# A transformer-and-experts layer on one core: the last expert place becomes a small one

## Chip, core and metric

The kernel runs on one core of a Trainium2 chip. The metric is device time in microseconds of one execution; lower is better. Engines: TensorE (PE, its weight loads PEld), VectorE (DVE), ScalarE (ACT), GpSimd (POOL), SyncE (SP, which issues most loads), and the core's 16 DMA engines.

## What is computed

One layer over 1024 tokens of width 1024: two token mixers (SSD and windowed attention), an output projection, and a mixture of 32 SwiGLU experts, each token in two of them, then a final RMSNorm. Only the end of it matters here:

```python
x = x + g1 * (jnp.concatenate([ssd_x, attn_x], axis=-1) @ w_out[layer])
h2 = rms_norm(x, norm2[layer]) * (1 + sc2) + sh2
...
def expert_block(args):
    xb, e = args
    return (jax.nn.silu(xb @ w_gate[e]) * (xb @ w_up[e])) @ w_down[e]
...
out = jax.ops.segment_sum(y_buf.astype(f32) * w_buf[:, None], tok_buf, num_segments=n_tok + 1)
...
x = x + g2 * moe_x.reshape(b, n_tok, d)
...
return rms_norm(x, norm_final)
```

The weights of an expert are 6 MB in f32 (gate, up, down); all 32 experts are read.

## The kernel before

After the mixers, `moe()` works through 32 *places*, one expert each. Which expert stands at which place is found on the chip: experts 0 to 2 keep places 0 to 2, the others are sorted by their count of tokens, and `ranks()` gives the smallest counts to the places in `HALVES`. Those are the *small* places: a block of up to 64 tokens, whose rows of 1024 are handled as two half rows of 512, so that 128 partitions are filled. A small place multiplies in plain f32 straight from the loaded weights `wf` (`half_gu` L1261, `half_down` L1285). All others are *full*: 128 tokens, and every weight tile is taken apart into two fp32r parts, `wh` by a cast on ScalarE (L179) and `wl` by a subtraction on VectorE (L180), with three matmuls for each product (`gu` L1320, `down` L1346). Tokens beyond a place's block go through a loop with a count found at run time (`moe_rest`).

Names of a place's steps: gathered tokens `xe` are transposed (`pxe`), gate and up go to PSUM `pgu`, ScalarE makes `sg` (`sgh` in a small place), VectorE the gated product `hg` (L1328; `hgh`, L1268), which is transposed (`phT`) into `hT`; down goes to `py`; VectorE scales it into `ye` (L1352; `yeh`, L1290), and POOL adds these rows into the tensor `acc` in HBM by an indirect DMA (L1356; L1294). `schedule()` writes the steps down: gate and up of place p stand between the down steps of place p-1, except where a place is apart (the last one is: place 30's down is done before place 31's gate and up). Within that, a scheduler orders each engine's instructions; an engine runs its own in that order.

Weights come in pieces of 1 MB, each place's six in the order of use, into two rings of 7 and 6 (`prefetch`); SyncE issues them in order and waits when no slot is free.

The end: `final()` gathers the rows of `acc` that the last place's tokens need (`ya`) and loads the eight blocks of 128 rows of `acc` (`yf`, SyncE). These wait until the adds of places 0 to 30 have landed. `final_rows()` normalises each block (square and sum on ScalarE L1538, root L1539, reciprocal L1540 and multiplication L1541 on VectorE) and writes it to the output (L1566). The last place is not added into `acc`: its product `ye` (L1568) is added to `ya` (L1569), normalised, and its rows are scattered over the written output (L1571), after the last of the eight writes.

Of the kernel before, what the change touches and what calls it, by code (L numbers as in the profile page):

```python
# [9 lines left out]
F32 = mybir.dt.float32  # L10
F32R = mybir.dt.float32r
BF = mybir.dt.bfloat16
I32 = mybir.dt.int32
AF = mybir.ActivationFunctionType
OP = mybir.AluOpType
AX = mybir.AxisListType

P = 128
D = 1024
NT = 1024  # L20
# [5 lines left out]
NE = 32  # L26
# [8 lines left out]
C_ID, C_SEL, C_COS, C_SIN, C_U, C_L, C_US, C_LS, C_ONE, C_BL, C_BR, C_SELB, C_IO, C_TOK, C_RP, C_HALF = (  # L35
    0, 128, 130, 386, 642, 770, 898, 1026, 1154, 1282, 1410, 1538, 1666, 1698, 1706, 1738)
# [20 lines left out]


FIXED, MID, REST = 3, 13, 14
HALVES = (3,) + tuple(range(4, NE - 1, 2))  # L60
H = 64

TS = NT + P
# [2 lines left out]
def ranks():  # L66

    r = list(range(FIXED)) + list(HALVES) + [p for p in range(FIXED, NE) if p not in HALVES and p != MID] + [MID]
    return [r.index(p) for p in range(NE)]
# [55 lines left out]
class Kern:  # L125
# [960 lines left out]
    def overflow(self):  # L1086
# [21 lines left out]

        nh = len(HALVES)
        v.tensor_scalar(cap, rank, FIXED - 0.5, float(H - P), op0=OP.is_ge, op1=OP.mult)  # L1110
# [74 lines left out]
    def half(self, b):  # L1185

        return b == NE or b in HALVES

# [230 lines left out]
    def moe(self):  # L1419
        blocks = list(range(MID + 1)) + [NE] + list(range(MID + 1, NE))  # L1420
        at = lambda p: [p, NE] if p == MID else [p]
        X, A, T, Y, Z, G = {}, {}, {}, {}, {}, {}
        done = 0
        add = lambda b: self.half_add(Z.pop(b), b) if self.half(b) else self.y_add(Z.pop(b), self.lst[:, b, :])

        def x_ahead(p):

            nonlocal done
            for b in at(p):
                k = blocks.index(b)  # L1430
                X[b] = self.half_x(k) if self.half(b) else self.x_t(k)
                for i in range(done, min(k + 3, NE + 1)):
                    if 4 <= i + 2 < NE + 1:
                        self.lst_load(blocks[i + 2])
                    self.gather(i, self.lst[:, blocks[i], :], blocks[i])
                done = min(k + 3, NE + 1)

        for i in range(3):
            self.lst_load(i)
        for i in range(2):  # L1440
            self.gather(i, self.lst[:, i, :])
        self.g2 = self.mod_load(self.mp, 3, "g2")
        self.g2h = self.mp([512], "g2h")
        for n in range(2):
            self.nc.sync.dma_start(out=self.g2h[n * H:n * H + H], in_=self.modd[3][None, n * 512:n * 512 + 512].to_broadcast([H, 512]))
        self.counts()
        self.lst_load(3)
        done = 2
        x_ahead(0)
        for t in self.steps:  # L1450
            k, p = t[0], t[-1] if len(t) == 2 else t[1] if len(t) > 2 else None
            if k == "gu":
                if t[2] == 0:
                    for b in at(p):
                        G[b] = self.bank2(name="pgu")
                wg, wu = self.chunk(p, 2 * t[2]), self.chunk(p, 2 * t[2] + 1)
                for b in at(p):
                    if self.half(b):
                        self.half_gu(t[2], X[b], wg[0], wu[0], G[b])
                    else:  # L1460
                        self.gu(t[2], X[b], wg[1], wu[1], G[b])
            elif k == "act":
                for b in at(p):
                    A[b] = (self.half_act if self.half(b) else self.act)(G.pop(b))
            elif k == "x":
                if p + 1 < NE:
                    x_ahead(p + 1)
            elif k == "hT":
                for b in at(p):
                    T[b] = (self.half_h if self.half(b) else self.h_t)(A.pop(b))  # L1470
                    Y[b] = self.bank2(name="py")
            elif k == "down":
                w = self.chunk(p, 8 + t[2])
                for b in at(p):
                    if self.half(b):
                        self.half_down(T[b], w[0], Y[b], t[2])
                    else:
                        self.down(T[b], w[1], Y[b], t[2])
            elif k == "y":
                for b in at(p):  # L1480
                    Z[b] = self.half_y(Y.pop(b), b) if self.half(b) else self.y_out(Y.pop(b), self.lst[:, b, :])
                    if p != REST - 1:
                        add(b)
            elif k == "rest":
                self.moe_rest()
                for b in list(Z):
                    add(b)
            elif k == "final":
                self.final()
            elif k == "last":  # L1490
                self.final_rows(Y.pop(p), self.lst[:, p, :])

    def moe_rest(self):

# [35 lines left out]
            self.y_add(self.y_out(py, lst, y), lst)  # L1530
        self.xe = xe

    def norm_out(self, y):

        nc, v = self.nc, self.nc.vector
        jk = self.fp([D], "junk", 2, BF)
        st = self.sml.tile([P, 2], F32, name="xss")
        nc.scalar.activation(jk, y, AF.Square, accum_out=st[:, 0:1])  # L1538
        nc.scalar.activation(st[:, 1:2], st[:, 0:1], AF.Sqrt, bias=self.eps, scale=1.0 / D)  # L1539
        v.reciprocal(st[:, 1:2], st[:, 1:2])  # L1540
        v.scalar_tensor_tensor(y, y, st[:, 1:2], self.nf, op0=OP.mult, op1=OP.mult)  # L1541

    def final(self):

        nc = self.nc
        self.wl.close()
        self.fp = self.pool("fin", "right")
        self.nf = self.fp([D], "nf")
        nc.scalar.dma_start(out=self.nf, in_=self.a["norm_final"].to_broadcast([P, D]))
        self.rowsy = self.fp([D], "ya")  # L1550
        nc.gpsimd.indirect_dma_start(
            out=self.rowsy, out_offset=None, in_=self.acc[:, :],
            in_offset=bass.IndirectOffsetOnAxis(ap=self.lst[:, NE - 1, 1:2], axis=0),
            bounds_check=NT + P - 1, oob_is_err=False)
        ys = [self.fp([D], "yf", 8) for _ in range(NBX)]
        for b in range(NBX):
            nc.sync.dma_start(out=ys[b], in_=self.acc[b * P:(b + 1) * P, :])
        self.ys = ys

    def final_rows(self, py, lst):  # L1560

        nc, v = self.nc, self.nc.vector
        outw = []
        for b in range(NBX):
            self.norm_out(self.ys[b])
            outw.append(nc.sync.dma_start(out=self.out[b * P:(b + 1) * P, :], in_=self.ys[b]))  # L1566
        y = self.mp([D], "ye", 2)
        v.scalar_tensor_tensor(y, py, lst[:, 2:3].bitcast(F32), self.g2, op0=OP.mult, op1=OP.mult)  # L1568
        v.tensor_tensor(y, y, self.rowsy, OP.add)  # L1569
        self.norm_out(y)  # L1570
        i = nc.gpsimd.indirect_dma_start(  # L1571
            out=self.out, out_offset=bass.IndirectOffsetOnAxis(ap=lst[:, 0:1], axis=0),
            in_=y, in_offset=None, bounds_check=NT - 1, oob_is_err=False)
        for o in outw:
            self.tc.add_manual_dep(i.ins, o.ins.name, mybir.DependencyInfo(mybir.DependencyClass.Sync, mybir.DependencyReason.DATA), reason="rows written twice")
        self.fp.close()
# [147 lines left out]
```

## Time and profile before

| | |
|---|---|
| median of 3 runs | 1316.91 us (1312.76 to 1318.18) |
| the profiled execution | 1317.32 us |
| its span, first to last instruction | 1315.2 us |
| TensorE busy | 1164.3 us (89%) |
| VectorE busy | 828.8 us (63%) |
| ScalarE busy | 598.2 us (45%) |
| HBM traffic over the span | 261 GB/s |
| granted TensorE clock, mean | 0.952 of full speed |

The profile is of one execution. Times in its rows count from the start of the span; a row's idle time in brackets names what ended the wait before it. In the expert stage many rows repeat a pattern with every pair of places.

### The profile page before, as it was taken

Reading aid. Unit: us, or ns where it says so; the run is one execution under the profiler, and the core shown is the slowest. Engines: PE = TensorE matmul, PEld = TensorE weight load, DVE = VectorE, ACT = ScalarE, POOL = GpSimd, SP = SyncE. Lnnn points to the kernel's source line nnn. Section 1 sums busy time; section 2 is a strip of 40 time slices with the busy share of each in tenths; the row PEclk is TensorE's granted clock in tenths of the full one; section 3 lists DMA queues with packets and bytes.
Section 4 is the critical chain, followed back from the end, with each engine's and each line's share of the span. In section 5 each row is a group of like instructions: output and inputs, shape, how many; then the busy total and the mean of one; then the engine's idle time right before and its main releaser. Section 6 shows DMA issues by size and latency. Waiting matters only on the chain. (4 is left out here: it accounts for less than half of the span.)

```text
span 1315.2 us, 18760 instructions
## 1 busy us (share of the span) xinstructions
PE 1164.3 (89%) x6628; PEld 853.0 (65%) x6628; DVE 828.8 (63%) x1396; ACT 598.2 (45%) x1064; POOL 341.2 (26%) x290
## 2 busy tenths in 40 slices
PE   5789999888888999899946999999899999999982
PEld 2678778778876666588744766655456666555551
DVE  1688885678956977555586855455345555555455
ACT  4643333265537776533342734344324443444344
POOL 0250000467623444211432121212112222122110
PEclk9889999989988999999977999999999999999996
DMA  9655644866423400395365899999869999999965
GB/s 338 251 201 184 211 137 133 255 194 215 154 69 100 139 31 9 118 355 178 120 248 169 311 374 412 406 394 380 307 229 412 395 405 405 389 389 386 360 203 224
DMA packets 104481, 335.02 MB, mean 255 GB/s; under 512 B 19533, under 2 KB 37965, under 8 KB 79809
## 3 DMA queue, kind: packets, MB, share of 16 engines
q1 hardware_dynamic: 94672, 314.78, 64.2%
q0 software_dynamic: 9136, 17.36, 5.3%
q10 hardware_dynamic: 576, 1.66, 0.3%
q8 instruction: 53, 0.87, 0.3%
q14 instruction: 44, 0.35, 0.1%
HBM read 299.74 MB, written 43.43 MB: 261 GB/s over the span
## 5 line engine op out<-in xcount | busy, mean ns | idle before, releaser
L180 DVE TENSOR_TENSOR wl<-wf,wh 128x1024 fp32r<-128x1024 f32 x204 | 241.7, 1220 | 86.0 <-ACT wh L179 82.6
L179 ACT CAST wh<-wf 128x1024 fp32r<-128x1024 f32 x204 | 204.8, 1050 | 136.3 <-PE pgu L1320 95.9
L1261 PE MATMUL pgu<-wf,xT 128*64 128x256 f32 x1024 | 135.0, 393 | 0.4 <-DVE yeh L1290 0.4
L1320 PE MATMUL pgu<-wl,xh 128*128 128x512 f32 x272 | 96.1, 418 | 17.1 <-DVE wl L180 17.1
L1261 PEld LDWEIGHTS pgu<-wf,xT 128*64 128x64 f32 x1024 | 73.6, 139 | 50.9 <-issue 15.2
L1320 PE MATMUL pgu<-wh,xh 128*128 128x512 f32 x272 | 96.1, 427 | 10.1 <-ACT wh L179 10.0
L466 PE MATMUL pzq<-xw,hxh 128*128 128x256 f32 x512 | 99.3, 293 | 0.0
L768 POOL TENSOR_SCALAR p<-p,sst 128x640 f32<-128x640 f32 (+1 forms) x32 | 66.0, 2065 | 101.3 <-DVE sst L765 53.7
L1320 PE MATMUL pgu<-wh,xl 128*128 128x512 f32 x272 | 88.8, 407 | 0.0
L1356 POOL DMA_INDIRECT acc<-ye,lst x16 | 34.2, 2140 | 198.8 <-DVE ye L1352 188.5
L1346 PE MATMUL py<-wh,hT 128*128 128x512 f32 x272 | 81.1, 407 | 3.4 <-ACT hT L1338 3.1
L466 PEld LDWEIGHTS pzq<-xw,hxh 128*128 128x128 f32 x512 | 82.4, 195 | 1.0 <-issue 0.2
L1320 PEld LDWEIGHTS pgu<-wl,xh 128*128 128x128 f32 x272 | 53.1, 195 | 39.1 <-DVE wl L180 26.1
L1320 PEld LDWEIGHTS pgu<-wh,xh 128*128 128x128 f32 x272 | 50.5, 195 | 40.7 <-ACT wh L179 25.3
L347 PE MATMUL pxb<-hxh,xw 128*128 128x512 f32 x256 | 76.4, 397 | 0.0
L466 PE MATMUL pzq<-xw,hxl 128*128 128x256 f32 x256 | 73.8, 288 | 0.0
L751 DVE TENSOR_REDUCE sst<-psc 128x1 f32<-128x640 f32 (+1 forms) x64 | 50.4, 789 | 27.5 <-PE psc L750 22.5
L1294 POOL DMA_INDIRECT acc<-yeh,hrow x16 | 35.4, 2215 | 114.7 <-DVE yeh L1290 97.1
L1285 PE MATMUL py<-wf,hTh 128*64 128x512 f32 x256 | 63.4, 613 | 0.9 <-ACT hTh L1278 0.9
L1346 PEld LDWEIGHTS py<-wh,hT 128*128 128x128 f32 x272 | 49.4, 190 | 21.8 <-ACT hT L1338 5.5
L1320 PEld LDWEIGHTS pgu<-wh,xl 128*128 128x128 f32 x272 | 53.6, 197 | 13.3 <-issue 2.4
L1309 ACT CAST xh<-pxe 128x512 fp32r<-128x512 f32 x34 | 19.5, 589 | 93.7 <-PE pgu L1320 57.5
(347 smaller groups left out, 2523.2 us busy)
## 6 DMA issues: line engine op xcount, KB each, us to landing
wf<-in_w_gate SPq DMA_DIRECT2D x64, 1024.0 KB
wf<-in_w_up SPq DMA_DIRECT2D x64, 1024.0 KB
wf<-in_w_down SPq DMA_DIRECT2D x64, 1024.0 KB
wa<-in_w_ada SPq DMA_DIRECT2D x48, 512.0 KB
R<-csd SPq DMA_DIRECT2D x16, 512.0 KB
xl<-xd SPq DMA_DIRECT2D x17, 256.0 KB
xt<-in_x SPq DMA_DIRECT2D x8, 512.0 KB
xf<-in_w_xbc SPq DMA_DIRECT2D x8, 512.0 KB
```

The source lines that it names most:

```text
L179: self.nc.scalar.copy(hi, src)
L180: (eng or self.nc.vector).tensor_tensor(lo, src, hi.bitcast(F32), OP.subtract)
L347: nc.tensor.matmul(px[s], w(wp, kc), self.hx(hp, kc, s, 512), start=st, stop=sp)
L466: nc.tensor.matmul(ps, self.hx(hp, kc, b // 4, P, (b % 4) * P), w(wp, kc), start=kc == 0 and hp + wp == 0, stop=kc == KC - 1 and hp == 1)
L751: v.tensor_reduce(mx, ps[:, o:512 + nl], AX.X, OP.max)
L768: (v if j % 2 else nc.gpsimd).tensor_scalar(p_, p_, den[:, j - i:j - i + 1], None, op0=OP.mult)
L1261: self.nc.tensor.matmul(pg[n * H:n * H + H, o:o + 256], xT[:, i0 + kk, a * H:a * H + H], w[:, kk * 512 + n * 256:kk * 512 + n * 256 + 256] ...
L1285: self.nc.tensor.matmul(py[n * H:n * H + H, 0:512], hT[:, i, a * H:a * H + H], w[:, n * 512:n * 512 + 512], start=f == 0, stop=f == 3)
L1294: self.nc.gpsimd.indirect_dma_start(out=self.acc.rearrange("t (a c) -> (t a) c", a=2), out_offset=bass.IndirectOffsetOnAxis(ap=self.hrow[: ...
L1320: nc.tensor.matmul(pg[:, n * 512:(n + 1) * 512], x[xp][:, k, :], w[wp][:, kk * 512:(kk + 1) * 512], start=k == 0 and xp + wp == 0, stop=k ...
L1346: nc.tensor.matmul(py[:, n * 512:(n + 1) * 512], hT[:, hp, f, :], wd[wp][:, n * 512:(n + 1) * 512], start=f == 0 and hp + wp == 0, stop=f ...
L1356: self.nc.gpsimd.indirect_dma_start(out=self.acc[:, :], out_offset=bass.IndirectOffsetOnAxis(ap=lst[:, 0:1], axis=0), in_=y, in_offset=Non ...
```

## The change

The last place, 31, becomes a small one. So that there are 15 small places as before, `HALVES` goes on in steps of two up to 24, and then 27, 29, 31 (before: up to 30). Places 25 and 26 are now both full, then small and full alternate to the end. The last place's rows are half rows: gathered from `acc` by half-row numbers `hr`, summed per half (`norm_half`), the two halves' sums added by a matmul with the matrix `pair`, multiplied with the half-width norm `nfh`, and scattered as half rows.

```diff
 FIXED, MID, REST = 3, 13, 14
-HALVES = (3,) + tuple(range(4, NE - 1, 2))
+HALVES = (3, 4, 6, 8, 10, 12, 14, 16, 18, 20, 22, 24, 27, 29, 31)
...
+    def norm_half(self, y):
+
+        nc, v = self.nc, self.nc.vector
+        jk = self.fp([512], "junkh", 1, BF)
+        st = self.sml.tile([P, 2], F32, name="xss")
+        nc.scalar.activation(jk, y, AF.Square, accum_out=st[:, 0:1])
+        ps = self.bank([1], name="psum", tag="B")
+        nc.tensor.matmul(ps, self.pair, st[:, 0:1], start=True, stop=True)
+        nc.scalar.activation(st[:, 1:2], ps, AF.Sqrt, bias=self.eps, scale=1.0 / D)
+        v.reciprocal(st[:, 1:2], st[:, 1:2])
+        v.scalar_tensor_tensor(y, y, st[:, 1:2], self.nfh, op0=OP.mult, op1=OP.mult)
...
-        self.rowsy = self.fp([D], "ya")
+        self.nfh, self.pair = self.fp([D // 2], "nfh"), self.fp([P], "pair")
+        for n in range(2):
+            nc.scalar.dma_start(out=self.nfh[n * H:n * H + H], in_=self.a["norm_final"][:, n * 512:n * 512 + 512].to_broadcast([H, 512]))
+
+            nc.vector.tensor_tensor(self.pair[:, n * H:n * H + H], self.ident[:, 0:H], self.ident[:, H:P], OP.add)
+        hr = self.fp([1], "hr", 1, I32)
+        nc.vector.tensor_scalar(hr, self.lst[:, NE - 1, 1:2], 2.0, self.C[:, C_HALF:C_HALF + 1], op0=OP.mult, op1=OP.add)
+        self.rowsy = self.fp([D // 2], "ya")
         nc.gpsimd.indirect_dma_start(
-            out=self.rowsy, out_offset=None, in_=self.acc[:, :],
-            in_offset=bass.IndirectOffsetOnAxis(ap=self.lst[:, NE - 1, 1:2], axis=0),
-            bounds_check=NT + P - 1, oob_is_err=False)
+            out=self.rowsy, out_offset=None, in_=self.acc.rearrange("t (a c) -> (t a) c", a=2),
+            in_offset=bass.IndirectOffsetOnAxis(ap=hr[:, 0:1], axis=0),
+            bounds_check=2 * (NT + P) - 1, oob_is_err=False)
...
-        y = self.mp([D], "ye", 2)
-        v.scalar_tensor_tensor(y, py, lst[:, 2:3].bitcast(F32), self.g2, op0=OP.mult, op1=OP.mult)
+        y = self.half_y(py, NE - 1)
         v.tensor_tensor(y, y, self.rowsy, OP.add)
-        self.norm_out(y)
+        self.norm_half(y)
         i = nc.gpsimd.indirect_dma_start(
-            out=self.out, out_offset=bass.IndirectOffsetOnAxis(ap=lst[:, 0:1], axis=0),
-            in_=y, in_offset=None, bounds_check=NT - 1, oob_is_err=False)
+            out=self.out.rearrange("t (a c) -> (t a) c", a=2),
+            out_offset=bass.IndirectOffsetOnAxis(ap=self.hrow[:, NE - 1:NE], axis=0),
+            in_=y, in_offset=None, bounds_check=2 * NT - 1, oob_is_err=False)
```

What it moves, engine by engine (names as above; the place a row belongs to is said in the sentence). VectorE before, from place 25's `hT` to the yeh of place 26, with place 27's splits around it:

```order
L1339 TENSOR_TENSOR hT<-phT,hT 128x512
L180 TENSOR_TENSOR wl<-wf,wh 128x1024 x2
L1352 SCALAR_TENSOR_TENSOR ye<-py,lst,g_6904 128x1024
L180 TENSOR_TENSOR wl<-wf,wh 128x1024
L1268 TENSOR_TENSOR hgh<-sgh,pgu 128x256
L180 TENSOR_TENSOR wl<-wf,wh 128x1024 x4
L1200 TENSOR_SCALAR hrow<-lst,C 128x1
L1290 SCALAR_TENSOR_TENSOR yeh<-py,lst,g2h 128x512
L180 TENSOR_TENSOR wl<-wf,wh 128x1024 x3
```

VectorE now, from `hg` of place 25 to `hg` of place 26:

```order
L1328 TENSOR_TENSOR hg<-sg,pgu 128x512
L180 TENSOR_TENSOR wl<-wf,wh 128x1024 x2
L1339 TENSOR_TENSOR hT<-phT,hT 128x512
L180 TENSOR_TENSOR wl<-wf,wh 128x1024 x4
L1200 TENSOR_SCALAR hrow<-lst,C 128x1
L180 TENSOR_TENSOR wl<-wf,wh 128x1024
L1352 SCALAR_TENSOR_TENSOR ye<-py,lst,g_6904 128x1024
L180 TENSOR_TENSOR wl<-wf,wh 128x1024 x3
L1310 TENSOR_TENSOR xl<-pxe,xh 128x512
L1328 TENSOR_TENSOR hg<-sg,pgu 128x512
```

Ten splits now stand between the gated products of two neighbouring full places, with `ye` of place 25 between the two splits of one gate-and-up step of place 26. ScalarE before, from place 31's casts (the last twelve of the kernel) to the first blocks' roots:

```order
L179 CAST wh<-wf 128x1024 x11
L1327 ACTIVATE sg<-pgu 128x512
L179 CAST wh<-wf 128x1024
L1538 ACTIVATE junk,xss<-yf 128x1024 x2
L1338 CAST hT<-phT 128x512
L1539 ACT_TABLE_LOAD
L1539 ACTIVATE xss<-xss,eps 128x1 x2
```

ScalarE now, from place 30's `sg` on; `sgh` and `hTh` are those of place 31:

```order
L1327 ACTIVATE sg<-pgu 128x512
L179 CAST wh<-wf 128x1024 x2
L1338 CAST hT<-phT 128x512
L1564 DMA nfh<-in_norm_final 64x512
L1267 ACTIVATE sgh<-pgu 128x256
L1278 COPY hTh<-phT 128x256
L1550 ACTIVATE junk,xss<-yf 128x1024
L1551 ACT_TABLE_LOAD
```

The squares of the blocks now stand behind all of place 31's work on ScalarE, and no cast of a weight comes after place 30's. VectorE at the end before, and then now:

```order
L1540 RECIPROCAL xss<-xss 128x1 x2
L1568 SCALAR_TENSOR_TENSOR ye<-py,lst,g_6904 128x1024
L1541 SCALAR_TENSOR_TENSOR yf<-yf,xss,nf 128x1024 x2
L1540 RECIPROCAL xss<-xss 128x1 x2
L1569 TENSOR_TENSOR ye<-ye,ya 128x1024
L1541 SCALAR_TENSOR_TENSOR yf<-yf,xss,nf 128x1024 x2
```

```order
L1268 TENSOR_TENSOR hgh<-sgh,pgu 128x256
L1290 SCALAR_TENSOR_TENSOR yeh<-py,lst,g2h 128x512
L1552 RECIPROCAL xss<-xss 128x1
L1587 TENSOR_TENSOR yeh<-yeh,ya 128x512
L1553 SCALAR_TENSOR_TENSOR yf<-yf,xss,nf 128x1024
L1552 RECIPROCAL xss<-xss 128x1
L1553 SCALAR_TENSOR_TENSOR yf<-yf,xss,nf 128x1024
```

The last place's product and its sum with `ya` stood between the last blocks' multiplications; they now stand ahead of the first one.

## Rows read from the trace of the kernel before

**Rows 1.** The page: the span, and TensorE's busy time and share.

```profile
span 1315.2 us, 18760 instructions
PE 1164.3 (89%) x6628; PEld 853.0 (65%) x6628; DVE 828.8 (63%) x1396; ACT 598.2 (45%) x1064; POOL 341.2 (26%) x290
```

**Rows 2.** By stretch: us; PE, PEld, DVE, ACT, POOL busy; clock; DMA share; GB/s.

```profile
1015.98:1047.55 31.57, 31.57 (x171) 21.00 (x170) 17.96 (x19) 15.46 (x19) 7.63 (x5) 1.00 1.02 400
...
1153.13:1188.81 35.68, 32.63 (x173) 20.77 (x172) 18.95 (x21) 14.95 (x20) 7.10 (x4) 1.00 1.02 387
...
724.20:742.80 18.60, 17.47 (x78) 13.86 (x77) 16.87 (x17) 13.82 (x17) 3.35 (x2) 1.00 0.81 284
```

**Rows 3.** The chain that ended last, in time: start us, us, what.

```profile
1288.08 7.35 PE py L1346 x24
...
1300.30 2.47 DVE yf L1541 x2
...
1302.80 2.72 DMA out<-yf
```

**Rows 4.** Waits of SyncE's queue over the last 215 us: total, times, longest.

```profile
SPq L1557 <- DMA acc<-yeh,hrow: 8.9, 1, 8.9
```

**Rows 5.** Timeline of VectorE: `hg` and `hgh` of places 23 to 29.

```profile
1138.51 0.68 DVE L1328 TENSOR_TENSOR hg<-sg,pgu 128x512 f32<-128x512 f32 x1
...
1174.18 0.68 DVE L1328 TENSOR_TENSOR hg<-sg,pgu 128x512 f32<-128x512 f32 x1
1188.81 0.42 DVE L1268 TENSOR_TENSOR hgh<-sgh,pgu 128x256 f32<-128x256 f32 x1 [1.61 <-ACT sgh L1267]
1211.29 0.68 DVE L1328 TENSOR_TENSOR hg<-sg,pgu 128x512 f32<-128x512 f32 x1
...
1248.53 0.68 DVE L1328 TENSOR_TENSOR hg<-sg,pgu 128x512 f32<-128x512 f32 x1
```

**Rows 6.** Timeline of VectorE: `hg` of the full places 1 and 2.

```profile
742.79 0.69 DVE L1328 TENSOR_TENSOR hg<-sg,pgu 128x512 f32<-128x512 f32 x1 [0.82 <-ACT sg L1327]
...
762.34 0.69 DVE L1328 TENSOR_TENSOR hg<-sg,pgu 128x512 f32<-128x512 f32 x1 [1.33 <-ACT sg L1327]
```

**Rows 7.** Timeline: products and adds of places 29 and 30, loads of `acc`.

```profile
1258.65 1.28 DVE L1352 SCALAR_TENSOR_TENSOR ye<-py,lst,g 128x1024 f32<-128x1024 f32 x1 [2.14 <-PE py L1346]
1260.21 1.55 POOL L1356 DMA_INDIRECT acc<-ye,lst  x1 [16.17 <-DVE ye L1352]
...
1268.85 2.28 POOL L1294 DMA_INDIRECT acc<-yeh,hrow  x1 [7.09 <-DVE yeh L1290]
...
1275.47 4.20 SPq L1557 DMA_DIRECT2D yf<-acc  x8
```

**Rows 8.** Timeline of TensorE: transposes, small matmuls, and (chain) 22 full ones.

```profile
1225.38 0.75 PE L1307 MATMUL pxe<-C,xe 128*128 128x128 f32 x4
...
1233.90 1.94 PE L1285 MATMUL py<-wf,hTh 128*64 128x512 f32 x8
...
1258.54 3.67 PE L1261 MATMUL pgu<-wf,xT 128*64 128x256 f32 x32
...
1253.38 5.23 PE py L1346 x22
```

**Rows 9.** Timeline of VectorE and ScalarE from place 31's `hg` on.

```profile
1285.21 0.68 DVE L1328 TENSOR_TENSOR hg<-sg,pgu 128x512 f32<-128x512 f32 x1
1285.36 1.06 ACT L1538 ACTIVATE junk<-yf 128x1024 bf16<-128x1024 f32 x1
...
1299.04 0.22 DVE L1540 RECIPROCAL xss<-xss 128x1 f32<-128x1 f32 x2
1299.17 1.21 DVE L1569 TENSOR_TENSOR ye<-ye,ya 128x1024 f32<-128x1024 f32 x1
```

**Rows 10.** Busy time by stretch (columns as in rows 2), at place 31's down.

```profile
1288.00:1291.30 3.30, 3.22 (x8) 2.55 (x9) 2.26 (x5) 3.27 (x7) 0.00 (x0) 0.54 0.25 99
```

**Rows 11.** DMA from 1275.4 to 1291.1 us, in 40 slices.

```profile
GB/s 0 0 104 136 386 386 303 428 386 438 230 344 355 376 365 376 365 417 365 397 386 428 386 438 397 449 407 438 386 449 386 449 397 355 84 31 0 0 0 0
```

More of the change, by code (lines that the diff above doesn't have):

```diff
@@ L1490, in moe @@
             elif k == "last":
-                self.final_rows(Y.pop(p), self.lst[:, p, :])
+                self.final_rows(Y.pop(p))
     def moe_rest(self):
@@ L1558, in final, with final_rows @@
         self.ys = ys
-    def final_rows(self, py, lst):
+    def final_rows(self, py):
         nc, v = self.nc, self.nc.vector
```

## The prediction

> **What bounds the kernel now.** I read the page first, then stretches of the expert stage, then the chain of waits at the end. TensorE is busy for 89% of the span [rows 1], so an order of places can gain only where TensorE waits, or after it has finished.
>
> In the expert stage a small and a full place alternate. The view by stretch [rows 2] goes from the gated product `hgh` of one small place to that of the next. A late pair takes 35.7 us, with TensorE busy for 32.6 of them. An earlier one needed 31.6 us and had no wait at all. The DMA engines are full in both, yet the chain's matmuls stand one behind the other: weights arrive well ahead. So what sets the pace is TensorE, plus a few waits for casts and splits on ScalarE and VectorE.
>
> The end is read from the chain in order of time [rows 3]. Matmuls of place 31 (the last are its down, 7.35 us) run into the eight multiplications `yf` on VectorE, the last output write (2.72 us), and the scatter of the patched rows, which is held until that write has landed. Two paths meet there. One is place 31 itself. The other starts at place 30: SyncE holds the eight loads of `acc` for 8.9 us until place 30's add has landed [rows 4], since a block can be normalised only when every expert but the last is in it. The reader is to see that the second path starts at place 30, not at place 31.
>
> **The change, part by part.** Up to the gate and up products of place 25 the engines' orders are those of before, so I start from its `hg` at 1174.18 us [rows 5].
>
> *Two full places in a row.* Place 26 was small and becomes full, behind full place 25. Before shows this twice, at places 0 to 2: the stretch from `hg` of place 0 to that of place 1 took 18.6 us [rows 2], and `hg` of place 2 followed 19.6 us behind that of place 1 [rows 6]. The order rows differ a little there: `ye` of place 25 now stands between the two splits that one step of place 26 needs, and TensorE waits for the second of them (1.28 us for `ye` [rows 7]). I take 20.0. The lower bound is 18.6. For the upper one I take the slow stretch from `hgh` of a small place to `hg` of the full one, 22.5 us [rows 2, 5], take out the small place's down (twice 1.94 us [rows 8]) and put in a full one at its slowest, 7.35 us [rows 3]: 26.0.
>
> *Two pairs, 27/28 and 29/30,* as before. The last three pairs took 35.7, 37.1 and 37.2 us from `hg` to `hg` [rows 5]; the mean is 36.7, two make 73.3 (71.3 to 74.5, or 63.1 if both ran like the 31.6 us pair). Place 31's input now needs four transposes instead of eight ahead of place 30; four take 0.75 us [rows 8], partly beside other waits: minus 0.6. `hg` of place 30: 1174.2 + 20.0 + 73.3 - 0.6 = 1266.9.
>
> *Place 30's down.* From `hg` of place 31 to the end of its down took 1295.4 - 1285.2 = 10.2 us [rows 3, 9]. Place 30 now takes that road, with two small matmuls (0.3 us) between. Sum 10.4, hence 1277.3. After the wait TensorE's clock was at 0.54 on the mean in 1288.0 to 1291.3, and 24 matmuls took 7.35 us; 22 such at full clock took 5.23 [rows 3, 8, 10]. So the lower bound is 8.5.
> The Trainium skill (page "TensorE: Matmul & The Clock Gate", section "What's actually happening") states that the throttled clock is the default and sustained activity releases it, so that an idle stretch is paid for again. By that rule the slow figure holds here, and the rows at 1288 us agree; by full clock the sum would be 1.9 us less.
>
> *The add of place 30 and the loads.* The product scaled into `ye` takes 1.28 us and POOL issues the add 1.56 us after it began; from issue to the first load of `acc` 6.6 us passed for a small place [rows 7]. With a gap of 0.1 that is 8.3: the loads go out at 1285.6. Before they went out at 1275.5, so this path starts 10.1 us later.
> The Trainium skill (page "DMA: Bandwidth & Descriptors", section "Anatomy of one DMA — SWDGE (gpsimd) path") fits such a DMA with 2.0 us plus the bytes at 436 GB/s. For half a megabyte an estimate from it is 3.2 us, and the sum would be 3.4 us less. The row shows 6.6 for less data, and I keep the row.
>
> *Loads to the last multiplication.* The loads and `ya` have moved after 36 of 40 slices of 15.7 us, 14.1 us [rows 11]. ScalarE is now free when they land (its last work for place 31 comes after 7.3 us of gate and up and two hand-overs, some 9 us after place 30's down; the first block comes 8.3 + 2.8, some 11), where before it was casting until 1285.4 [rows 9]. VectorE takes longest: eight multiplications and reciprocals at (2.47 + 0.22)/2 = 1.35 us [rows 9] with 0.05 between, 11.2 us. In its new order the add of `ya` stands ahead of them all. I take `ya`, half as many bytes as before, as landed 7.5 us after the first load (bounds 3, when the first half megabyte has moved, and 14, all bytes [rows 11]); the add costs half of 1.21 us [rows 9]. 7.5 + 0.6 + 11.2 = 19.3, hence 1304.9. Bounds are 17 (the last block at 14.1, its square, 1.06 [rows 9], root and multiplication) and 25.8. Before it was 27.3 (1275.5 to 1302.8), since casts, place 31's `ye` and full-width `ya` lay between.
> The new matmul with `pair`, the half-width square and root lie beside these; the reciprocal of the last rows stands ahead of the last multiplication and may cost a few tenths.
>
> *From there to the end,* 1302.8 to 1315.2, 12.4 us: last write, scatter, drain [rows 3]. The scatter has half rows now, at the same issue; I take it as equal. End: 1317.3.
>
> *Removed.* Place 31's full gate, up and down leave the end. A small place takes about 13 us (twice 3.67 of gate and up, twice 1.94 of down [rows 8], hand-overs), all beside the add and the loads: it is done some 13 us after place 30's down, and its rows wait for `ya`, some 16 us after it. `pair` and `hr`, three small VectorE operations, and the two `nfh` loads lie in waits. Weight bytes are equal, and the loads of place 31's down, which stand ahead of `acc` on SyncE, wait for place 30's splits and go out before its down ends.
>
> **Sum.** 1317.3 against 1315.2 us: 2.1 us later, +0.16%. The profiled execution took 1317.32, 2.1 more than its span and 0.4 above the median of 1316.9; so 1319.0 as a median. What is taken out behind place 30 (about 8 us in the loads, and place 31's full matmuls) is nearly all given back, because a full place has moved ahead of the point from which the loads start.
>
> **The rivals.**
> *Slower: the second full place jams.* Place 26's splits compete with those of place 25's down. VectorE was busy for 16.9 of 18.6 us in such a stretch before [rows 2], and with `ye` between two splits TensorE may wait at each step. At 26.0 us instead of 20.0 the time is 1325. It decides from 24.5, where the sum passes +0.5%. For it: the late order already waits where the early one did not. Against: places 0 to 2 show 19.6 at most. 11%.
> *Slower: `ya` is late.* The eight multiplications now queue behind its add on VectorE. If it lands with the last block, 14 us after the first load, the time is 1325.5; it decides from 12. Against: its bytes are halved and it is issued with the first loads. 4%.
> *Faster: the end follows the last place.* If the loads' path were not the later one, a small place at the end saves what a full one takes more, 27.7 us (from 1267.7, some 1.2 ahead of place 30's add [rows 7], to 1295.4 [rows 3]) less 13. The loads leaving at 1275.5 as now would then give 1275.5 + 19.3 + 12.4 + 1.7 (the 2.1 less 0.4) = 1309. For it: the chain runs through place 31 now. Against: place 30's add cannot land as early with a full place more ahead. 4%.
> *Faster: the pace of the 31.6 us pair comes back* in pairs 27/28 and 29/30: 1309. Against: in the changed order one split stands ahead of `hgh` and `yeh` between two others, as in the slow pairs of before. 4%.
> *Nothing moves,* because the pieces cancel exactly, is within my forecast; the order listing shows that the change does move them.
>
> **How the numbers follow.** My case, within 0.5% (6.6 us, about what a measurement of this kernel can tell from no change), has 77%. Faster 8%, slower 15%. My case's own range is 1314.5 to 1323.5: the bounds of the stretch (-1.4, +2), of the pairs (-2, +1.2), of the down (-1.9) and of the last part (-2.3, +2) do not all fall on one side. The range for 8 in 10 reaches part of the way into the cases on either side: 1311.5 to 1326.
>
> **What would show it.** `hg` of places 25 and 26 some 20 us apart; `hg` of place 30 near 1267; `acc` loads issued near 1285.6; ScalarE waiting for the first block; the last `yf` multiplication near 1305; 12.4 us from there. It is wrong if the loads go out before 1280, if the two full places take over 24 us, or if VectorE waits for `ya`.

## The result, and the profile after

The changed kernel took 1326.82 us (median of 6 runs, 1322.4 to 1330.1) against 1316.83: ratio 1.0069, 95% interval 1.0046 to 1.0091. Twelve further runs of it (below) gave 1.0036 (1.0013 to 1.0059). Weighted by runs the two give 1.0047: slower, by about the bound of 0.5% that the prediction set, where 1319.0 and +0.16% were forecast. The median of the first six lies 0.8 us above the upper end of the range, that of the twelve inside it.

The page of the changed kernel, against [rows 1]:

```profile
span 1325.6 us, 18772 instructions
PE 1168.7 (88%) x6630; PEld 855.6 (65%) x6630; DVE 827.9 (62%) x1399; ACT 598.8 (45%) x1064; POOL 340.8 (26%) x290
```

The matmuls are nearly the same in number (6630 against 6628). Of the 10.4 us more, 4.4 are longer busy time of TensorE, at a mean granted clock of 0.945 instead of 0.952, and 6.0 are time without a matmul. The view by stretch of the changed kernel (columns as in [rows 2]) goes from `hgh` of small place 24 to `hg` of full places 25, 26, 28 and 30, and on to place 30's add:

```profile
1151.77:1173.71 21.94, 19.66 (x76) 12.38 (x76) 12.95 (x13) 10.76 (x14) 2.70 (x2) 0.92 1.01 366
1173.71:1196.54 22.83, 19.96 (x86) 15.51 (x87) 15.09 (x15) 12.04 (x15) 4.78 (x3) 0.93 1.00 365
1196.54:1234.46 37.92, 34.87 (x172) 21.31 (x170) 19.05 (x21) 15.03 (x20) 5.70 (x3) 0.95 0.92 343
1234.46:1271.88 37.42, 33.73 (x156) 20.77 (x152) 20.97 (x24) 16.33 (x21) 4.58 (x2) 0.91 0.72 249
1271.88:1283.95 12.07, 10.43 (x48) 7.02 (x50) 4.93 (x5) 2.34 (x3) 0.00 (x0) 0.86 0.40 147
```

The rows of the kernel before that follow on its 35.68 us pair of [rows 2], to `hgh` of places 28 and 30 and to the add:

```profile
1188.81:1225.91 37.10, 34.05 (x173) 21.82 (x172) 18.95 (x20) 14.93 (x20) 7.10 (x4) 0.95 1.02 393
1225.91:1262.68 36.77, 33.25 (x164) 20.80 (x163) 17.79 (x19) 13.96 (x18) 3.84 (x2) 0.95 0.76 267
1262.68:1268.85 6.17, 4.82 (x20) 1.67 (x20) 1.44 (x3) 4.15 (x5) 0.00 (x0) 1.00 0.94 295
```

The two full places in a row stand 22.83 us apart, not 20.0. The timeline of VectorE and TensorE there shows why:

```profile
1184.96 1.23 DVE L180 TENSOR_TENSOR wl<-wf,wh 128x1024 fp32r<-128x1024 f32 x1 [1.14 <-ACT wh L179]
1186.60 1.28 DVE L1352 SCALAR_TENSOR_TENSOR ye<-py,lst,g 128x1024 f32<-128x1024 f32 x1 [0.42 <-PE py L1346]
1187.80 3.49 DVE L180 TENSOR_TENSOR wl<-wf,wh 128x1024 fp32r<-128x1024 f32 x3
1189.07 0.50 PE L1320 MATMUL pgu<-wl,xh 128*128 128x512 f32 x1 [1.83 <-DVE wl L180]
```

VectorE does one split of place 26's step, then waits 0.42 us for place 25's last matmul, does `ye`, and only then the second split; TensorE stands still for 1.83 us. Behind it, from 1190.0 to 1192.5 us, two matmuls take 1.05 us instead of the 0.62 from 1193.3 on: a while at the lower clock (0.93 on the mean in this stretch).

The end, on the timeline (GpSimd, VectorE, SyncE): place 30's add, `ya` and the blocks.

```profile
1283.95 1.55 POOL L1356 DMA_INDIRECT acc<-ye,lst  x1 [16.42 <-DVE ye L1352]
1290.12 3.80 SPq L1576 DMA_DIRECT2D yf<-acc  x8
1298.79 0.69 DVE L1587 TENSOR_TENSOR yeh<-yeh,ya 128x512 f32<-128x512 f32 x1 [2.29 <-DMA ya<-acc,hr]
1299.40 1.28 DVE L1553 SCALAR_TENSOR_TENSOR yf<-yf,xss,nf 128x1024 f32<-128x1024 f32 x1
1308.94 1.28 DVE L1553 SCALAR_TENSOR_TENSOR yf<-yf,xss,nf 128x1024 f32<-128x1024 f32 x1
1316.84 1.04 POOL L1589 DMA_INDIRECT out<-yeh,hrow  x1 [24.89 <-issue]
```

The chain that ended last, in time, has the last write at twice its former length (2.72 us in [rows 3]):

```profile
1290.97 7.53 DMA yf<-acc
...
1308.97 1.27 DVE yf L1553
1310.26 5.43 DMA out<-yf
```

GB/s of the DMA engines in 40 slices, first the changed kernel from 1290 to 1316 us, with what was moved in them, then the kernel before from 1275 to 1306 us:

```profile
GB/s 0 82 252 378 403 403 290 296 353 359 334 397 397 410 429 416 410 416 416 403 435 416 416 416 416 422 435 403 410 422 410 410 429 410 410 151 25 25 19 0
DMA packets 2385, 8.66 MB, mean 333 GB/s; under 512 B 272, under 2 KB 272, under 8 KB 2384
```

```profile
GB/s 0 42 254 344 412 344 333 381 375 391 391 412 412 412 412 418 418 312 26 0 0 37 402 338 402 370 396 407 349 16 137 407 412 391 5 248 412 412 280 0
```

Before, the loads of `acc` are over before the first write, and the writes have gaps in which VectorE is awaited. Now loads and writes run into one another, some 400 to 430 GB/s without a gap: at the end the writes wait for the DMA engines, no longer for VectorE. The Trainium skill (page "DMA: Bandwidth & Descriptors", section "Where 436 GB/s comes from") has about 435 GB/s as the ceiling of the fabric and says that for transfers between HBM and SBUF some 358 bind; the rows agree with the first and not with the second.

### The profile page after: what moved, and what is told of

It is laid out like the page before. It is cut to its first block, busy times and chain, and to the rows that moved or that the text cites. A ratio compares the mean times of both kernels' runs of the same rounds, so it can differ in the third digit from the quotient of the medians.

```text
span 1325.6 us, 18772 instructions
## 1 busy us (share of the span) xinstructions
PE 1168.7 (88%) x6630; PEld 855.6 (65%) x6630; DVE 827.9 (62%) x1399; ACT 598.8 (45%) x1064; POOL 340.8 (26%) x290
## 5 line engine op out<-in xcount | busy, mean ns | idle before, releaser
L1320 PE MATMUL pgu<-wl,xh 128*128 128x512 f32 x272 | 98.1, 424 | 15.5 <-DVE wl L180 15.4
L1320 PEld LDWEIGHTS pgu<-wh,xl 128*128 128x128 f32 x272 | 54.9, 202 | 13.7 <-issue 2.4
L1346 PEld LDWEIGHTS py<-wh,hT 128*128 128x128 f32 x272 | 49.3, 190 | 22.3 <-issue 5.9
```

What stands on the lines that cost most here:

```text
L1320: nc.tensor.matmul(pg[:, n * 512:(n + 1) * 512], x[xp][:, k, :], w[wp][:, kk * 512:(kk + 1) * 512], start=k == 0 and xp + wp == 0, stop=k ...
L1346: nc.tensor.matmul(py[:, n * 512:(n + 1) * 512], hT[:, hp, f, :], wd[wp][:, n * 512:(n + 1) * 512], start=f == 0 and hp + wp == 0, stop=f ...
```

## Experiments

**1. The order alone,** last place full.

```diff
-HALVES = (3,) + tuple(range(4, NE - 1, 2))
+HALVES = (3, 4, 6, 8, 10, 12, 14, 16, 18, 20, 22, 24, 27, 29, 30)
```

> The kernel before with the order of places alone changed: small places 3, 4, 6 to 24, 27, 29, 30; the last place stays full, and places 25 and 26 are full in a row as in the change. My theory: the change lost time at two unrelated places, some 3 us where full 25 and 26 stand in a row (a wait of 1.8 us for a split and a stretch at half clock behind it) and the rest at the end, behind the last place's new form; so this order alone costs 1 to 4 us: 1318 to 1321, with hg of 25 and 26 some 22.8 us apart. First rival, the order alone costs all: 1326. Second rival, all is lost at the end and nothing in the order: 1317.

Measured: 1319.76 us, 1.0015 (0.9998 to 1.0033). This lies within what my theory said. Its stretches from `hgh` of place 24 to the gated products of 26, 28 and 30:

```profile
1153.01:1194.70 41.69, 36.55 (x161) 25.74 (x163) 28.05 (x29) 22.80 (x28) 6.07 (x4) 1.00 1.01 369
1194.70:1237.37 42.67, 35.86 (x172) 21.62 (x170) 18.44 (x21) 14.88 (x19) 6.73 (x4) 0.92 0.89 334
1237.37:1263.63 26.26, 25.31 (x174) 16.63 (x170) 9.75 (x11) 6.47 (x10) 3.12 (x2) 1.00 0.88 315
```

The first stretch took 41.7 us at full clock, against 44.8 (21.94 + 22.83) in the changed kernel with the same instructions. TensorE was busy for 36.6 us in the one and 39.6 (19.66 + 19.96) in the other: these 3.1 us are its clock. `hg` of 25 and 26 stand 21.3 us apart here (1173.43 to 1194.70), not 22.8. In all 110.6 us, 1.1 more than before (35.68 + 37.10 + 36.77). This order alone does not cost what the change costs. It is not quite the order of the change, though: small 29 and 30 stand in a row, and TensorE waits 3.9 us for gathered rows (1206.4 to 1210.3), so that from `hg` of place 26 to `hgh` of place 27 it took 22.3 us, 15.3 in the changed kernel.

**2. The pair of full places elsewhere,** last place small.

```diff
-HALVES = (3, 4, 6, 8, 10, 12, 14, 16, 18, 20, 22, 24, 27, 29, 31)
+HALVES = (3, 4, 6, 8, 10, 12, 15, 17, 19, 21, 23, 25, 27, 29, 31)
```

> The changed kernel with the two full places in a row moved from 25/26 to 13/14 (small: 3, 4, 6 to 12, 15, 17 to 31). Place 14's gate and up stand behind all of place 13's down there, so that no step of the one stands between steps of the other. My theory: the 3 us of places 25/26 go and the end stays as it is: 1322 to 1324, pairs at 37 us up to place 30. First rival, the order costs all: about 1317. Second rival, the end costs all: 1326 to 1328.

Measured: 1318.25 us, 0.9987 (0.9972 to 1.0003): less than my theory had, and the time of the first rival. That does not show the order at 25/26 to be the whole cause. With the pair at 13/14 a wait of TensorE is absent that the kernel before (3.6 us) and the changed one (3.6 and 3.8) both have: it is for the gathered rows of place 14, which is small there and full here (the first row in experiment 12 shows it). From `hg` of place 11 to `hgh` of place 12 this kernel took 15.1 us, the kernel before 21.1 and the changed one 21.3. These 6 us have nothing to do with the last place; with them, this kernel would lie some 4 us above the kernel before.

**3. One operation moved.** In the changed kernel `ye` of place 25 is emitted a step later and ordered behind the step's second split.

```diff
-                    st += down[2:4] + [("y", p - 1)]
+                    st += down[2:4] + ([] if p == 26 else [("y", p - 1)])
+                if p and not apart and j == 2 and p == 26:
+                    st += [("y", p - 1)]
...
+                    if (p + 1) == 26:
+                        self.tc.add_manual_dep(self.last_y.ins, self.last_split.ins.name, ...)
```

> The changed kernel with one operation of VectorE moved: ye of place 25 is made to stand behind the second split of place 26's third gate-and-up step, instead of between its two splits. My theory: the wait of 1.83 us of TensorE for that split goes, and most of the stretch at half clock behind it; hg of 25 and 26 stand 19.5 to 21 us apart instead of 22.8, and the time is 1323.5 to 1325.5. Rival, casts and splits of two full places are too many for the stretch, wherever ye stands: the distance stays at 22 to 23 us and the time at 1327.

Measured: 1322.13 us, 1.0020 (1.0002 to 1.0037). The stretch from `hg` of place 25 to that of 26, and from `hg` of place 30 to its add:

```profile
1178.64:1198.98 20.34, 19.17 (x90) 14.51 (x91) 15.00 (x15) 12.05 (x15) 4.41 (x3) 1.00 1.00 375
...
1271.53:1282.05 10.52, 8.88 (x48) 6.27 (x50) 4.93 (x5) 2.33 (x3) 0.00 (x1) 1.00 0.52 185
```

20.34 us instead of 22.83, at full clock: the wait was `ye`, as my theory said. Only 0.9 us of the difference is the wait, though. With `ye` in its old place the stretch took 21.2 us in experiments 4, 6 and 11, where the clock had not fallen; the other 1.6 us are the clock. Experiment 6 from `hgh` of place 24 to `hg` of 26, to be held against 44.77 us in the changed kernel:

```profile
1152.45:1194.10 41.65, 36.50 (x161) 25.74 (x163) 28.02 (x29) 22.80 (x28) 7.49 (x5) 1.00 1.02 374
```

The time, 1.0020, is not clearly apart from that of experiment 5. The second row of experiment 3 is a surprise: place 30's down, 90 us later, ran at full clock here and took 10.5 us to the add instead of 12.07, with the same matmuls.

**4. Half the output bytes.** Only the left half of each block is written.

```diff
-outw.append(nc.sync.dma_start(out=self.out[b * P:(b + 1) * P, :], in_=self.ys[b]))
+outw.append(nc.sync.dma_start(out=self.out[b * P:(b + 1) * P, 0:512], in_=self.ys[b][:, 0:512]))
```

> The changed kernel with only the left 512 columns of each block written to the output (the right half of the rows is left out), nothing else changed. My theory: from the first load of acc to the last write the DMA engines are the bound, 8.7 MB in some 21 us, so with 2.1 MB less the last write lands 3 to 5 us earlier and the time is 1322 to 1324; from the last yf multiplication to the end of the span some 12.5 us instead of 15.4. Rival, the longer last write is a fixed time of its own, behind ScalarE and VectorE that set the pace of the blocks: within 1 us of 1327.

Measured: 1324.85 us, 1.0040 (1.0016 to 1.0064). Its last multiplication and its scatter on the timeline:

```profile
1313.60 1.28 DVE L1553 SCALAR_TENSOR_TENSOR yf<-yf,xss,nf 128x1024 f32<-128x1024 f32 x1
...
1318.12 1.04 POOL L1589 DMA_INDIRECT out<-yeh,hrow  x1 [21.00 <-issue]
```

From the last multiplication's start to the scatter 4.5 us, against 7.9 in the changed kernel (1308.94 to 1316.84) and 6.4 in the profile of experiment 5. Part of this is that a write of half the bytes is shorter by itself: whole writes that meet no loads took 5.3 us (experiment 8), so that the crowd on the DMA engines is worth 1.1 to 2.6 us. The time as a whole does not show it clearly (1.0040 against 1.0036 to 1.0069), and it lies above the 1322 to 1324 of my theory; the stretch shows it.

**5. The changed kernel again.**

> The changed kernel once more, unaltered, beside its variants. Its time was the median of six runs that went from 1322.4 to 1330.1. My theory, that those six stand for it: 1.005 to 1.008 of the kernel before. Rival, the six fell on the slow side of a scatter that every variant has: 1.002 to 1.004, and then the gain of moving ye (1.0020) is smaller than it looked.

Measured: 1325.38 us, 1.0036 (1.0013 to 1.0059): inside the rival's range. Its stretches from `hgh` of place 24 to `hg` of 26, 28 and 30:

```profile
1156.53:1201.31 44.78, 39.63 (x161) 28.05 (x163) 28.03 (x28) 22.80 (x28) 7.49 (x5) 0.92 0.99 358
1201.31:1239.25 37.94, 34.89 (x172) 21.30 (x170) 19.05 (x22) 15.04 (x20) 5.70 (x3) 0.96 0.93 343
1239.25:1274.29 35.04, 30.86 (x156) 19.17 (x152) 20.97 (x25) 16.34 (x21) 4.57 (x2) 1.00 0.76 264
```

The 44.8 us of the first stretch came again; the last pair took 35.0 at full clock where it took 37.4 before at 0.91.

**6. `ya` behind the blocks.**

```diff
-        v.tensor_tensor(y, y, self.rowsy, OP.add)
+        one = self.fp([1], "one")
+        v.tensor_scalar(one, self.ys[NBX - 1][:, 0:1], 0.0, 1.0, op0=OP.mult, op1=OP.add)
+        v.scalar_tensor_tensor(y, y, one, self.rowsy, op0=OP.mult, op1=OP.add)
```

> The changed kernel with the sum of the last place's product and ya made to wait for the last yf multiplication (a factor of one, made from that block, stands in it), so that the first block's multiplication no longer waits some 2.3 us for ya. My theory: the DMA engines, with 8.7 MB of reads and writes behind the loads of acc, bound the end, so the writes start some 3 us earlier but the last one lands at most 1.5 us earlier: 0 to 1.5 us gained. Rival, VectorE's eight multiplications in a row set the end: 2.5 to 3 us gained.

Measured: 1326.97 us, 1.0057 (1.0035 to 1.0079): nothing gained. On its timeline, the loads, the first multiplication and the scatter:

```profile
1285.39 4.01 SPq L1576 DMA_DIRECT2D yf<-acc  x8
...
1292.07 1.28 DVE L1553 SCALAR_TENSOR_TENSOR yf<-yf,xss,nf 128x1024 f32<-128x1024 f32 x1
...
1310.76 1.04 POOL L1591 DMA_INDIRECT out<-yeh,hrow  x1 [23.55 <-issue]
```

The first multiplication starts 6.7 us behind the loads instead of 9.3 (8.6 in experiment 5), but the scatter comes 25.4 us behind them, between the 26.7 and the 24.5 (1292.20 to 1316.73) of the changed kernel's two profiles. The 2 to 2.6 us won at the front do not come out at the back: VectorE's wait for `ya` is real and not the bound.

**7. `ye` behind the split everywhere,** in the kernel before: the edit of experiment 3 for every full place whose gate and up stand between another place's down steps.

> The kernel before (last place full, order as before) with every ye and yeh that stands between the two splits of a full place's third gate-and-up step made to stand behind the second split. My theory: the waits of about 1.1 us of TensorE for that split, in nearly every pair, go (some 10 of them, 11.8 us in all from 800 us on), and the time is 1306 to 1312, faster than both kernels. Rival, the wait only moves to the next cast or split: within 2 us of before.

Measured: 1306.44 us, 0.9902 (0.9880 to 0.9924), faster than both kernels. Its stretches from `hgh` of place 24 to that of 26, 28 and 30, and to place 30's add:

```profile
1146.17:1180.51 34.34, 32.37 (x173) 20.84 (x172) 18.95 (x21) 14.94 (x20) 7.00 (x4) 1.00 1.02 387
1180.51:1214.85 34.34, 32.37 (x173) 20.84 (x172) 18.95 (x21) 14.94 (x20) 7.75 (x4) 1.00 1.01 396
1214.85:1249.09 34.24, 31.80 (x164) 19.67 (x163) 17.88 (x19) 14.04 (x18) 3.84 (x2) 1.00 0.97 372
1249.09:1258.05 8.96, 6.07 (x24) 2.52 (x25) 4.23 (x5) 4.15 (x5) 0.00 (x1) 1.00 0.93 294
```

Each late pair lost 1.3 to 2.8 us against the 35.7, 37.1 and 36.8 of the kernel before, and TensorE stayed at full clock. Its waits for a split from 800 us on fell to 6.1 us; the first row is this kernel's, the second the kernel before's (to 1268 us):

```profile
PE pgu L1320 <- DVE wl L180: 6.1, 10, 1.3
```

```profile
PE pgu L1320 <- DVE wl L180: 11.8, 15, 1.1
```

**8. Blocks that need no add,** loaded from `h2` instead of `acc`.

```diff
-            nc.sync.dma_start(out=ys[b], in_=self.acc[b * P:(b + 1) * P, :])
+            nc.sync.dma_start(out=ys[b], in_=self.h2d[b * P:(b + 1) * P, :])
```

> The changed kernel with the eight blocks of the end loaded from the normalised tokens h2 in place of acc (the output is then not the layer's: the sum over the experts is left out of it), so that they need not wait for place 30's add; only ya still does. My theory: the path over place 30's add, the loads and the eight blocks is what ends the kernel; without it the last rows end it, some 8 us behind ya, and the time is 1309 to 1313. Rival, something else bounds the end (place 31's own matmuls, the scatter): 1323 or more.

Measured: 1324.00 us, 1.0034 (1.0014 to 1.0054). My theory fell: the blocks' path is not what ends the kernel by itself. On its timeline:

```profile
1298.38 0.69 DVE L1587 TENSOR_TENSOR yeh<-yeh,ya 128x512 f32<-128x512 f32 x1 [2.16 <-DMA ya<-acc,hr]
...
1308.54 1.28 DVE L1553 SCALAR_TENSOR_TENSOR yf<-yf,xss,nf 128x1024 f32<-128x1024 f32 x1
...
1313.89 1.04 POOL L1589 DMA_INDIRECT out<-yeh,hrow  x1 [17.98 <-issue]
```

All eight multiplications now wait for `ya` alone, which also hangs on place 30's add. From the last multiplication to the scatter 5.3 us, not 7.9: with the loads gone from there, the writes are not crowded. The test is not quite clean: place 30's add took 9.2 us (1284.77 to 1293.96), 3 more than the 6.2 in the changed kernel, and `ya` waits for it.

**9. The changed kernel with `ye` behind everywhere.**

> The changed kernel (last place small, 25 and 26 full in a row) with every ye and yeh made to stand behind the second split of the step, as in the run that brought the kernel before to 0.990. My theory: what the change loses has two parts, waits of TensorE with stretches at half clock behind them, which this takes out, and some 4 us that stay (a full place more ahead of place 30's add, and writes that crowd behind the loads at the end); so it stays 3 to 6 us behind that run: 0.993 to 0.995 of before. Rival, waits and clock were all of it: 0.990. Second rival, moving ye helps only the old order: 1.000 or more.

Measured: 1314.12 us, 0.9961 (0.9942 to 0.9981), 0.6% behind experiment 7: more than I expected. The stretches that answer to those of experiment 7 (`hgh` of 24, `hg` of 26, 28 and 30, add):

```profile
1146.31:1186.12 39.81, 37.11 (x165) 25.85 (x167) 27.95 (x28) 22.79 (x28) 7.77 (x5) 1.00 1.00 396
1186.12:1220.75 34.63, 32.65 (x168) 20.38 (x166) 19.04 (x21) 15.03 (x20) 5.96 (x3) 1.00 1.02 385
1220.75:1254.41 33.66, 30.56 (x156) 19.26 (x152) 20.97 (x24) 16.33 (x21) 4.58 (x2) 1.00 0.92 336
1254.41:1266.46 12.05, 10.41 (x46) 7.00 (x48) 4.93 (x5) 2.34 (x3) 0.00 (x0) 0.86 0.54 180
```

This is the cleanest pair, since both ran at full clock up to place 30. The product of place 30 comes 5.2 us later (108.1 against 102.9) and its add 3.1 us more (12.05 against 8.96); from the add to the end 40.8 us (1266.46 to the span of 1307.3) against 44.0 (1258.05 to 1302.0), 3.1 us given back. That leaves 5.2 us in these profiles; the runs say 7.8. Of the 3.1 us to the add some 1.5 are clock (0.86 here; experiment 10 took 10.55 us at full clock). Moving `ye` brought the changed kernel about as much as the kernel before, so these waits are not what sets the two apart.

**10. Experiment 9 with the pair at 13/14.**

> The changed kernel with the two full places in a row moved to 13/14 and every ye and yeh behind the second split. My theory: a small last place by itself costs nothing and gains little, so it comes within 3 us of the kernel before with ye behind: 0.988 to 0.992. Rival, the crowded writes at the end stay as a loss: 0.993 or more.

Measured: 1308.40 us, 0.9925 (0.9902 to 0.9948), between the two bounds; no clear verdict against experiment 7. Like experiment 2 it lacks the wait for the rows of place 14: from `hg` of place 11 to `hgh` of place 12 it took 15.1 us, experiment 7 21.9. Without these 6.8 us this kernel would be some 10 us behind experiment 7, not 3. Its last pair and the stretch to place 30's add:

```profile
1216.47:1252.54 36.07, 33.46 (x156) 20.87 (x152) 20.96 (x24) 16.33 (x21) 4.59 (x2) 0.91 0.84 309
1252.54:1263.09 10.55, 8.91 (x46) 6.26 (x48) 4.93 (x5) 2.33 (x3) 0.00 (x1) 1.00 0.60 202
```

**11. Blocks and `ya` both free,** the edits of experiments 6 and 8 together.

> The changed kernel with both holds at the end taken away: the blocks come from h2 in place of acc (the sum over the experts is left out of the output) and the sum with ya stands behind the eight multiplications. Each of the two alone gained 0 to 1.5 us. My theory: they are two paths of equal length from place 30's add, so that only both together help; ScalarE's eight squares behind place 31's hTh set the end then: the first write some 5 us earlier after hg of place 30 than in the changed kernel, and 1319 to 1322, that is 0.9995 to 1.0015 of before. Rival, neither is the bound: 1.003 or more.

Measured: 1322.77 us, 1.0023 (1.0000 to 1.0046): less than expected and, as a time, not clearly different from either alone. The stretch does show a gain: from place 30's add to the end of the span 35.1 us, against 37.8 in experiment 8 and 41.7 and 39.3 in the changed kernel's two profiles. The timeline shows the next hold in line, the last place itself:

```profile
1295.55 0.75 DVE L1290 SCALAR_TENSOR_TENSOR yeh<-py,lst,g2h 128x512 f32<-128x512 f32 x1 [4.72 <-PE py L1285]
...
1296.41 1.28 DVE L1553 SCALAR_TENSOR_TENSOR yf<-yf,xss,nf 128x1024 f32<-128x1024 f32 x1
```

Place 31's `yeh` stands ahead of the multiplications on VectorE, so they cannot start before its down is done. In the changed kernel `yeh` came at 1294.6, the first block's reciprocal at 1296.3 and `ya` at 1298.8: three holds within some 4 us.

**12. Pair at 13/14, small 29 and 30, last place full, `ye` behind everywhere.**

> The kernel before with ye and yeh behind the second split everywhere, its last place full, and the small places 3, 4, 6 to 12, 15, 17 to 29 and 30: full places in a row at 13/14, small ones in a row at 29/30. My theory: of the gain that the pair at 13/14 brought to the changed kernel, 3.8 us were one wait of TensorE for the gathered rows of place 14 (a small one there before), which has nothing to do with places 25 and 26; so this order gains 3 to 5 us on the run with ye behind everywhere: 0.986 to 0.988. Rival, the pair at 13/14 helped only because it took the place of the one at 25/26: 0.990.

Measured: 1306.34 us, 0.9904 (0.9882 to 0.9925), as experiment 7. The time is the rival's, but its reason is not shown. The wait for the rows of place 14 did go, and some 6 us with it: 15.1 us from `hg` of place 11 to `hgh` of place 12, against 21.9 in experiment 7. Another wait for gathered rows came instead (1197.1 to 1200.3), ahead of place 27, as in experiment 1, which also has small 29 and 30 in a row: from `hg` of place 26 to `hgh` of place 27 it took 21.4 us, where a full place and the small one behind it (25 and 26) take 14.6 in experiment 7. Gain and loss cancel. The first row is the changed kernel's in experiment 5 from 900 to 1020 us, the second this kernel's from 800 to 1262 us:

```profile
PE pxe L1250 <- DMA xe<-h2d,hrow: 3.8, 1, 3.8
```

```profile
PE pxe L1250 <- DMA xe<-h2d,hrow: 3.2, 1, 3.2
```

## Why the prediction was right or wrong

The mechanism was right: what a small last place takes out behind place 30 is given back, because a full place has moved ahead of the add from which the end starts. The gain behind place 30 came out smaller than in the sum, and the delay ahead of the add larger. Two terms of the sum were too small: the two full places in a row and the last write. By its steps, in the profiled execution (1325.6 against the forecast 1317.3, 8.3 us):

- *Two full places in a row, 20.0 us:* 22.8, in both profiles of the changed kernel. The text named `ye` between two splits and TensorE's wait, and then priced it at 0.4 us above the early places of [rows 6]; the wait was 1.83 us. At full clock the stretch took 21.2 to 21.3 us (experiments 1, 4, 6 and 11), so the term was 1.2 too small, 0.9 of it the wait (experiment 3: 20.3), and the clock adds 1.6 in both profiles of the changed kernel. Experiment 3 shows that `ye` is the cause of the wait; why the clock fell in some runs and not in others is open, since all of them have the wait.
- *Two pairs, 72.7 with the transposes off:* 75.3 in the first profile, 73.0 in experiment 5. Right within the scatter, which is clock: TensorE was without a matmul for 6.7 us in the first and 7.2 in the second.
- `hg` of place 30 was forecast for 1266.9 and came at 1271.88: all but 0.1 of the 5.0 us from these two and an earlier start of 0.5.
- *Place 30's down 10.4, add and loads 8.3:* 10.5 to `ye` (1282.4) and 7.7 to the loads. Right. The Trainium skill's rule on the throttled clock (page "TensorE: Matmul & The Clock Gate", section "What's actually happening") agreed in the changed kernel (0.86 in the stretch to the add), but in experiment 3 the same stretch ran at full clock: it is not sure to be paid. The estimate from the Trainium skill's fit (page "DMA: Bandwidth & Descriptors", section "Anatomy of one DMA — SWDGE (gpsimd) path"), 3.2 us for the add, was too low by the trace: 6.2 us from its issue to the first load (1283.95 to 1290.12). The row was the better price.
- *Loads to the last multiplication, 19.3:* 20.1 (1290.12 to 1310.2). `ya` came after 8.7 us, not 7.5, and VectorE waited for it, which the text named as a sign of error. Experiment 6 shows no gain from taking this wait away.
- *From there to the end, 12.4:* 15.4, and 13.9 in experiment 5. This step failed. It is 12.4 to 12.5 us in all four kernels with a full last place (before, 1, 7, 12), 13.7 to 15.4 in those with a small one and the end unaltered (changed, 2, 3, 5, 9, 10), and 12.8 where the loads are out of the way (8, 11). The sum took the length of the last write from a kernel whose writes had the DMA engines to themselves. Having compressed loads and writes into 26 us, I did not add up their bytes: 8.7 MB at some 410 GB/s are 21 us. Experiments 4 and 8 show it from two sides. Of the 8 us that the text counted as taken out of the loads, 7.2 came (27.3 to 20.1), and 3.0 of them were lost again here.

The likeliest case, "within 0.5%", missed by little or held by little: 1.0069 and 1.0036. The rival "the second full place jams" had the right place, but 22.8 us stay below its 24.5. The second rival's sign, VectorE's wait for `ya`, came without its price (8.7 us, where it decides from 12). The rival by which the end follows the last place was wrong: experiments 8 and 11 show three paths of nearly one length at the end, so that no single cut reaches 1309.

Whether each half of the change is free by itself, as experiments 1 and 2 seem to say, is not shown. The orders of 2, 10 and 12 lack the wait for the rows of place 14, worth some 6 us that the kernel before pays too; those of 1 and 12 have one at place 27 that the changed kernel does not have. Reckoned with these stretches, the small last place is behind in every order: some 4 us in 2 against before, 7.8 in 9 against 7 and some 10 in 10 against 7. This is an estimate from stretches; no run takes that wait away by itself.

Open: how much of the 0.4 to 0.7% is the clock. One and the same stretch differed by 1.5 to 3.1 us between profiles with its clock.

## What to carry to other kernels

Making the last step smaller moves its work ahead of whatever the end waits for: find the event from which the end's loads start, and price what is moved ahead of it. Where an end is pressed together, add up the bytes of its loads and writes against the rate in the rows; a write's length from a looser schedule no longer holds. The larger gain lay in an ordinary wait: on an engine that works in order, a scaling that waits for TensorE stood between the two halves of what TensorE needs next, in nearly every pair; behind them it brought 1%.

## What the runs showed of the hardware

TensorE's clock followed such waits unevenly. In the kernel before, a late pair ran at 1.00 [rows 2] and the next at 0.95, with 3.05 us without a matmul in either (35.68 less 32.63, 37.10 less 34.05); in experiment 7, with `ye` behind the split and 1.97 to 2.44 us without a matmul, three late pairs ran at 1.00, but with the same edit the last pair of experiment 10 ran at 0.91. The same instructions took 44.8 us at 0.92 in two profiles of the changed kernel and 41.7 at 1.00 in experiments 1 and 6. Twelve runs of one kernel (experiment 5) went from 1317.5 us at a mean clock of 0.954 to 1332.5 at 0.939, so a spread of 1.1% comes with the clock. The Trainium skill (page "TensorE: Matmul & The Clock Gate", section "What's actually happening") says that the ramp of the clock varies from run to run of one kernel. The runs agree: the mean clock of one kernel differs from run to run.

An add of 0.5 MB into HBM took 6.2 us from issue to the release of the loads, and 9.2 us beside eight loads of the same size (experiment 8's chain, 1284.77 to 1293.96).
